# Placing four groups of value products behind chosen projection matmuls, and storing the last output row in equal halves

## The chip, the cores and the metric

The program runs on one core of one Trainium2 chip. The metric is the device time of one execution in microseconds (us). The kernel before takes 954.18 us, the median of three runs that lie between 954.12 and 955.09 us. Below, PE is the matmul engine (TensorE), DVE is VectorE, ACT is ScalarE, POOL is GpSimd and SP is SyncE, which here only issues transfers.

## What is computed

One layer of a hybrid decoder over 1040 tokens (16 learned ones ahead of 1024), with a model width of 1024, in float32:

```python
u = rmsnorm(h, g_pre_mix);  z = u @ w_in            # 1024 -> q 512 | k 128 | v 128 | x 512 | y 512
# B: sliding-window attention, window 128, 8 heads of 64, 2 key/value heads, a sink per head
s = q k^T / 8, masked;  p = exp(s - max) / (sum + exp(sink - max));  attn = p v
# A: causal conv(4) on x, then a gated linear recurrence
r, i = sigmoid(xc w_a + b_a), sigmoid(xc w_x + b_x)
a = exp(-8 r softplus(-lam));  h_t = a h_(t-1) + sqrt(1 - a^2) i xc;  rec = gelu(y) h
h = h + rmsnorm(concat(attn, rec) @ w_out)
h = h + rmsnorm(relu(rmsnorm(h) @ w_ff1)^2 @ w_ff2);  return h[16:]
```

## The kernel before

**Numbers and tiles.** Each float32 operand is split into a high and a low part (`split`, lines 94 to 101: a cast on ACT at line 96 and a subtraction on DVE at line 99). A product is then three matmuls (`mm3`, lines 123 to 132: line 125 high by high, line 128 high by low, line 129 low by high). `project` (lines 257 to 270) multiplies one 128-column chunk of `w_in` with the tokens piece by piece, in a PSUM bank with the tag `acc`, of which there are two. `ALL` has four pieces (272, 256, 256 and 256 tokens, 24 matmuls each), `REAL2` two of 512 tokens.

**Attention and its filling.** The loop at line 752 goes over four pairs of heads j and two halves of the tokens. Each turn issues the scores of (j, half), then one projection as filling (`next_fill`), and then `attend` for the (j, half) of the turn before. The fillings come in the order q1, x1, q2, x2, q3, x3, y0, y1, y2, y3; q stands for queries, x for the input of the recurrence and y for its gate. All but the first few are given a low priority, and so they fill PE where nothing more urgent is ready. After the loop come y2 as filling and `attend(3, 1)`; after the gates of the recurrence (`gates`, line 797) comes y3.

`attend` (lines 642 to 681) works on two groups bp = 0 and 1 of two blocks of 128 tokens each; the text calls a group (j, half, bp). Per group: four transposes of the weights on PE (line 649), the split into `mh` and `ml` on ACT and DVE, four mask selections on POOL (line 653, two of `mh` and two of `ml`), then the **value products**, six matmuls at line 663: one of 512 columns from `mh` and one from `ml`, then two and two of 256 columns (128 for each head). Their result is taken from the PSUM bank by two copies on ACT (line 678) and two additions on DVE (line 679).

**What orders the work.** Each engine runs its instructions in a fixed order. A planner makes that order when the program is built: it takes what is ready by its own reckoning, by priority, which is the order of the source with the lags that the kernel adds. `behind(name, ins)` (line 106) adds a rule to it: `ins` is put later than `name`, with no semaphore where both are on one engine. Before the change one group is placed by such a rule, (3, 1, 1): all six of its matmuls stand behind the first matmul of the third `mm3` of y1 (`begun[1][2]`, lines 668 and 669). `begun[c]` holds the first matmul of each `mm3` of y fill c.

**The conv and y0.** `conv` (line 686) does the causal convolution on DVE: one instruction at line 689 and three at line 694 for chunk 3. Fill y0 is copied out of its two banks by ACT (line 723) into a tile with the tag `d`, which the input of the last convolution holds until its last instruction at line 694.

**The end.** The last product of the feed-forward part ends with `finish_late` (line 1422) for four rows of 128 tokens. Per row: the sum at line 1430 on DVE is preceded by an addition (`combine`, line 1030), ACT squares and takes the root (lines 1393 and 1440), DVE takes the reciprocal and scales the row in two pieces (line 1444), and each piece is stored, one by SP and one by ACT (line 1447). For rows 0 to 2 the pieces are columns 512 to 1023 (SP) and 0 to 511 (ACT). For row 3, the last, they are 256 to 1023 (768 columns, SP) and 0 to 255 (ACT).

Of the kernel before, what the change touches and what calls it, by code (L numbers as in the profile page):

```python
# [17 lines left out]
D = 1024  # L18
# [5 lines left out]
NPAIR = 4  # L24
# [13 lines left out]
def hybrid_layer(  # L38
# [6 lines left out]
    nc = tc.nc  # L45
    x, out = x[0], out[0]
# [11 lines left out]
    def slot(tag, shape, dt=F32):  # L58
        uid[0] += 1
        return slab.tile(shape, dt, tag=tag, name=f"{tag}{uid[0]}", bufs=bufs[tag])  # L60

    def pair(tag, shape):
        return slot(tag, shape, F32R), slot(tag, shape, F32R)

    def bank(tag, shape=(P, 512)):
        uid[0] += 1
        return ps.tile(list(shape), F32, tag=tag, name=f"ps_{tag}{uid[0]}")

    def f32(ap):
        return ap.bitcast(F32)  # L70
# [23 lines left out]
    def split(hi, lo, src, eng=None):  # L94
        if eng is None:
            nc.scalar.copy(hi, src)  # L96
        else:
            eng.tensor_copy(hi, src)
        low = nc.vector.tensor_tensor(lo, src, f32(hi), op=ALU.subtract).ins  # L99
        mark[0] = low.name  # L100
        return low
# [4 lines left out]
    def behind(name, *inss):  # L106
        for ins in inss:
            tc.add_manual_dep(
                ins, name,
                mybir.DependencyInfo(  # L110
                    mybir.DependencyClass.NoSync, mybir.DependencyReason.DATA
                ),
                reason="order",
            )
# [8 lines left out]
    def mm3(dst, lhs, rhs, start, stop):  # L123
        (lh, ll), (rh, rl) = lhs, rhs
        ins = nc.tensor.matmul(  # L125
            dst, lh, rh, start=start, stop=False, skip_group_check=True
        ).ins
        nc.tensor.matmul(dst, lh, rl, start=False, stop=False, skip_group_check=True)  # L128
        last_mm[0] = nc.tensor.matmul(  # L129
            dst, ll, rh, start=False, stop=stop, skip_group_check=True  # L130
        ).ins.name
        return ins
# [124 lines left out]
    def project(w, pieces, sink, begun=None):  # L257
        wh, wl = w
        for t0, n in pieces:
            acc = bank("acc")  # L260
            for kc in range(KC):
                uh, ul = u[kc]
                ins = mm3(
                    acc[:, :n], (wh[:, kc, :], wl[:, kc, :]),
                    (uh[:, t0 : t0 + n], ul[:, t0 : t0 + n]),
                    kc == 0, kc == KC - 1,
                )
                if begun is not None:
                    begun.append(ins)
            sink(acc[:, :n], t0, n)  # L270
# [11 lines left out]
    ALL = [(0, 272), (272, 256), (528, 256), (784, 256)]  # L282
# [41 lines left out]
    last = [None, None]  # L324
# [120 lines left out]
    def new_q():  # L445

        q = pair("b", [P, T])

        def sink_q(acc, t0, n):
            c = slice(t0 - NMETA, t0 - NMETA + n)  # L450
            for h in range(2):
                r, o = HALF[h], HALF[1 - h]
                q_made[:] = split_scaled(q[h][r, c], q[h][o, c], acc[r], HD ** -0.5)

        return q, sink_q

    def new_x(tag="d", c=0):
        xr = slot(tag, [P, TT])
        y = slot("d", [P, TT]) if c == 2 else None

        def sink_x(acc, t0, n):
            nc.scalar.copy(xr[:, t0 : t0 + n], acc)
            if y is not None:
                nc.scalar.activation(
                    y[:, t0 : t0 + n], acc, AF.Identity,
                    scale=prm[:, c, 3:4], bias=prm[:, c, 4:5],
                )

        return xr, sink_x, y
# [172 lines left out]
    def attend(j, half, pairs):  # L642
        g = j // 2
        o_ = slot("e", [P, 512])
        for bp, sn in enumerate(pairs):
            mh, ml = pair("c", [P, 4, 2, P])
            pt = bank("pt", (P, 4, P))
            for k in range(4):
                nc.tensor.transpose(pt[:, k, :], sn[:, k, 0:P], ident)
            split(mh[:, :, 1, :], ml[:, :, 1, :], pt)  # L650
            for m in (mh, ml):
                for side, op, sign in ((0, ALU.is_gt, 1), (1, ALU.is_ge, -1)):
                    nc.gpsimd.affine_select(  # L653
                        out=m[:, :, side, :], in_=f32(m)[:, :, 1, :],
                        pattern=[[0, 4], [-sign, P]], compare_op=op, fill=0.0,
                        base=0, channel_multiplier=sign,
                    )
            po = bank("o", (P, 2, 256))
            mhv, mlv = (m.rearrange("p (h i) s q -> p h (i s q)", h=2) for m in (mh, ml))

            def av(v, oc, n, pc, first, last):
                for k, m in enumerate((mhv, mlv)):
                    ins = nc.tensor.matmul(  # L663
                        po[:, :, oc : oc + n], v, m[:, :, pc : pc + n],
                        start=first and k == 0, stop=last and k == 1,
                        skip_group_check=True,
                    ).ins
                    if (j, half, bp) == (NPAIR - 1, 1, 1):
                        behind(begun[1][2].name, ins)

            b = 4 * half + 2 * bp
            av(vk[g][:, b, :], 0, 256, P, True, False)
            av(vm[:, g, :] if b == 0 else vk[g][:, b - 1, :], 0, P, 0, False, False)
            av(vk[g][:, b + 1, :], P, P, 3 * P, False, True)
            c = slice(256 * bp, 256 * bp + 256)
            for h in range(2):
                r, o = HALF[h], HALF[1 - h]
                nc.scalar.copy(o_[r, c], po[o, h, :])
                nc.vector.tensor_tensor(o_[r, c], po[r, h, :], o_[r, c], op=ALU.add)
        ah, al = at[half][j // 2]  # L680
        split(ah[:, j % 2, :], al[:, j % 2, :], o_)
# [4 lines left out]
    def conv(c, xr, tag="d", y=None):  # L686
        if y is None:
            y = slot(tag, [P, TT])
            nc.vector.tensor_scalar(
                y, xr, prm[:, c, 3:4], prm[:, c, 4:5], op0=ALU.mult, op1=ALU.add  # L690
            )
        for k in (2, 1, 0):
            s = 3 - k
            nc.vector.scalar_tensor_tensor(
                y[:, s:], xr[:, : TT - s], prm[:, c, k : k + 1], y[:, s:],
                op0=ALU.mult, op1=ALU.add,
            )
        xc[c] = y

    ys = [None] * NLRU  # L700
    begun = {}

    def fill_q(j):
        def run(w):
            q, sink = new_q()
            project(w, REAL2, sink)
            qs[j] = q
        return run

    def fill_x(c):  # L710
        def run(w):
            xr, sink, y = new_x(c=c)
            project(w, ALL, sink)
            conv(c, xr, "b" if c == 3 else "d", y)
        return run

# [250 lines left out]
    def out_banks(t):  # L967
        tag = ("pt", "o", "acc", "s", "pt", "acc", "s", "pt")[t]
        return [bank(tag), bank(tag)]
# [190 lines left out]
    for t in range(8):  # L1160
        po = pos[t] if t < 4 else out_banks(t)
# [227 lines left out]
    COLS = (slice(0, 512), slice(512, 1024))  # L1389
# [32 lines left out]
    def finish_late(j, y, parts):  # L1422

        h, o, ssq = halves[j]
        acc = facc["0", j]
        for k, c in enumerate(parts):
            yield k
            last = combine(acc[:, c], y[k], acc[:, c], ALU.add).name
            part = squares(y[k], acc[:, c], k)
            scaled = combine(o[:, c], acc[:, c], gffn_b[:, c], ALU.mult)  # L1430
            if len(parts) == 1:
                behind(last, *held)
                held.clear()
            else:
                behind(scaled.name, held.pop(0))
            if k < len(parts) - 1:
                nc.vector.tensor_tensor(ssq, ssq, part, op=ALU.add)
        root = small.tile([P, 1], F32, name="root", tag="root")
        rs = small.tile([P, 1], F32, name="rs", tag="rs")
        lut(root, part, AF.Sqrt, bias=ssq)  # L1440
        nc.vector.reciprocal(rs, root)
        cut = 256 if j == 3 else 512
        for c, eng in zip((slice(cut, D), slice(0, cut)), (nc.sync, nc.scalar)):
            held.append(nc.vector.scalar_tensor_tensor(
                o[:, c], o[:, c], rs, h[:, c], op0=ALU.mult, op1=ALU.add
            ).ins)
            eng.dma_start(out[j * P : (j + 1) * P, c], o[:, c])
# [102 lines left out]
```

## Time and profile before

| what | value |
| --- | --- |
| median of 3 runs | 954.18 us |
| the profiled execution | 953.82 us |
| its span, first to last instruction | 952.1 us |
| attention with its fillings | up to about 187 us |
| gates, recurrence | about 187 to 240 us |
| output projection, feed-forward | about 225 us to the end |

The profiled execution spent 1.7 us outside its span. All times of day in the text are microseconds from the start of the span. A row of the timeline gives the start, the duration, the engine, the line, the operation, "out<-in" by tile names without their numbers, the shapes, how many instructions are merged in the row, and in brackets how long the engine sat idle before it and what ended that. PE's matmuls overlap, and so the distance between the starts of two rows is what PE spends on one: 0.12 us for 256 columns and 0.23 us for 512. PEq, ACTq and SPq are the engines' own instruction queues.

### The profile page before, as it was taken

To read this page: it belongs to the slowest core of one execution; us is meant where nothing else is said; L and a number is where in the kernel's file an instruction comes from. 1 tells how busy PE (TensorE), PEld (TensorE's weight loads), DVE (VectorE), ACT (ScalarE), POOL (GpSimd) and SP (SyncE) were. 2 spreads that over 40 slices of the span, in tenths; PEclk is the share of its full clock that TensorE was granted. 3 is DMA by queue.
4 is the path that set the end of the run, shared out by engine and by line. 5 is a ranking of instruction groups with operands and counts; after the bars stand their busy time and mean duration, and the time that the engine had idled before them with its cause. 6 is when DMAs were issued, how large, how long until landed. Compare 5 with 4: busy or idle time off the path is not lost.

```text
span 952.1 us, 12444 instructions
## 1 busy us (share of the span) xinstructions
PE 941.1 (99%) x4677; PEld 785.6 (83%) x4677; DVE 681.4 (72%) x966; ACT 499.8 (52%) x824; POOL 154.3 (16%) x196
## 2 busy tenths in 40 slices
PE   9999999999999999999999999999999999999996
PEld 8999999878888877888888888888888888888885
DVE  6679998878966776665655466567667676779874
ACT  7556676579345554433555575663533343445441
POOL 2115665600021100000101001101121100003020
PEclk9999999999999999999999999999999999999999
DMA  8121101203246466675656457645677665556512
GB/s 291 52 54 36 42 5 34 89 24 110 67 168 185 134 208 212 181 262 176 221 177 199 155 185 230 202 157 145 164 178 176 181 217 201 180 194 155 131 46 89
DMA packets 85628, 140.76 MB, mean 148 GB/s; under 512 B 5784, under 2 KB 49064, under 8 KB 85568
## 3 DMA queue, kind: packets, MB, share of 16 engines
q1 hardware_dynamic: 75104, 108.64, 35.6%
q0 software_dynamic: 9600, 29.36, 12.1%
q10 hardware_dynamic: 864, 1.97, 0.6%
q8 instruction: 37, 0.61, 0.3%
q14 instruction: 23, 0.19, 0.1%
HBM read 115.70 MB, written 23.07 MB: 146 GB/s over the span
## 4 chain that ended last, share of the span: by engine, by line
PE 94%; DVE 2%; POOL 2%; ACT 1%; DMA 0%; issue 0%; SPq 0%; DVEq 0%; ACTq 0%; POOLq 0%
PE ps_acc L125 11%; PE ps_acc L128 11%; PE ps_acc L129 11%; PE ps_pt L125 7%; PE ps_pt L129 7%; PE ps_pt L128 6%; PE ps_s L125 6%; PE ps_s L129 6%; PE ps_s L128 6%; PE ps_o L128 5%; PE ps_o L125 5%; PE ps_o L129 5%; POOL c L653 1%; PE ps_o L663 1%; PE ps_o L1004 1%; PE ps_s L602 1%
## 5 line engine op out<-in xcount | busy, mean ns | idle before, releaser
L96 ACT CAST ws<-raw 128x1024 fp32r<-128x1024 f32 (+1 forms) x64 | 65.4, 1022 | 100.7 <-PE ps_o L128 47.1
L99 DVE TENSOR_TENSOR ws<-raw,ws 128x1024 fp32r<-128x1024 f32 (+1 forms) x65 | 78.2, 1203 | 38.0 <-ACT ws L96 37.9
L125 PE MATMUL ps_acc<-a,ws 128*128 128x256 f32 (+2 forms) x256 | 85.7, 335 | 0.0
L129 PE MATMUL ps_acc<-a,ws 128*128 128x256 f32 (+2 forms) x256 | 85.0, 333 | 0.0
L128 PE MATMUL ps_acc<-a,ws 128*128 128x256 f32 (+2 forms) x256 | 84.9, 331 | 0.0
L99 DVE TENSOR_TENSOR b<-b,b 128x1024 fp32r<-128x1024 f32 (+2 forms) x48 | 57.5, 1198 | 27.4 <-PE ps_o L128 22.2
L96 ACT CAST ws<-e 128x1024 fp32r<-128x1024 f32 x41 | 42.9, 1047 | 65.1 <-PE ps_o L128 37.7
L99 DVE TENSOR_TENSOR ws<-e,ws 128x1024 fp32r<-128x1024 f32 x41 | 50.1, 1222 | 26.7 <-ACT ws L96 26.7
L96 ACT CAST b<-b 128x1024 fp32r<-128x1024 f32 (+2 forms) x48 | 49.5, 1030 | 37.6 <-DVE b L1030 34.6
L653 POOL TENSOR_SCALAR_AFFINE_SELECT c<-c 128x512 fp32r<-128x512 f32 x64 | 56.2, 901 | 24.0 <-ACT c L96 20.3
L125 PEld LDWEIGHTS ps_acc<-a,ws 128*128 128x128 f32 x256 | 48.2, 188 | 5.2 <-issue 0.9
L178 POOL TENSOR_TENSOR rs<-ms,half_pow 128x1 f32<-128x1 f32 x26 | 19.4, 750 | 203.2 <-DVE ms L174 202.0
L129 PEld LDWEIGHTS ps_acc<-a,ws 128*128 128x128 f32 x256 | 48.2, 188 | 4.9
L128 PEld LDWEIGHTS ps_acc<-a,ws 128*128 128x128 f32 x256 | 48.1, 188 | 4.3 <-issue 0.2
L125 PE MATMUL ps_acc<-ws,b 128*128 128x512 f32 (+1 forms) x120 | 46.3, 386 | 0.0
L129 PE MATMUL ps_acc<-ws,b 128*128 128x512 f32 (+1 forms) x120 | 46.2, 385 | 0.0
L128 PE MATMUL ps_acc<-ws,b 128*128 128x512 f32 (+1 forms) x120 | 46.1, 384 | 0.0
L128 PE MATMUL ps_pt<-ws,b 128*128 128x512 f32 x112 | 44.0, 393 | 0.0
L125 PE MATMUL ps_pt<-ws,b 128*128 128x512 f32 x112 | 44.0, 394 | 0.0
L129 PE MATMUL ps_pt<-ws,b 128*128 128x512 f32 x112 | 43.9, 392 | 0.0
L125 PE MATMUL ps_s<-ws,b 128*128 128x512 f32 x110 | 43.3, 395 | 0.0
L129 PE MATMUL ps_s<-ws,b 128*128 128x512 f32 x110 | 43.3, 393 | 0.0
(438 smaller groups left out, 2740.5 us busy)
## 6 DMA issues: line engine op xcount, KB each, us to landing
raw<-in_w_ff_dram SPq DMA_DIRECT2D x51, 512.0 KB, 4.3
e<-in_w_ff_dram SPq DMA_DIRECT2D x33, 512.0 KB, 4.2
m<-in_w_ff_dram SPq DMA_DIRECT2D x16, 512.0 KB, 4.7
raw<-in_w_in_dram SPq DMA_DIRECT2D x12, 512.0 KB, 5.3
d<-in_w_ff_dram SPq DMA_DIRECT2D x12, 512.0 KB, 4.6
s_dram<-d POOLq DMA_DIRECT2D x12, 512.0 KB, 3.9
raw<-in_w_ff_dram POOLq DMA_DIRECT2D x10, 512.0 KB, 5.7
e<-in_w_ff_dram POOLq DMA_DIRECT2D x9, 512.0 KB, 5.7
```

Source lines behind the costliest of these rows:

```text
L96: nc.scalar.copy(hi, src)
L99: low = nc.vector.tensor_tensor(lo, src, f32(hi), op=ALU.subtract).ins
L125: ins = nc.tensor.matmul(dst, lh, rh, start=start, stop=False, skip_group_check=True).ins
L128: nc.tensor.matmul(dst, lh, rl, start=False, stop=False, skip_group_check=True)
L129: last_mm[0] = nc.tensor.matmul(dst, ll, rh, start=False, stop=stop, skip_group_check=True).ins.name
L178: last_pow[0] = nc.gpsimd.tensor_tensor(rs[:n], ms[:n], half_pow[:n], op=ALU.pow).ins.name
L602: nc.tensor.matmul(dst, q[h][:, c], lo, start=False, stop=True, skip_group_check=True,)
L653: nc.gpsimd.affine_select(out=m[:, :, side, :], in_=f32(m)[:, :, 1, :], pattern=[[0, 4], [-sign, P]], compare_op=op, fill=0.0, base=0, cha ...
L663: ins = nc.tensor.matmul(po[:, :, oc : oc + n], v, m[:, :, pc : pc + n], start=first and k == 0, stop=last and k == 1, skip_group_check=Tr ...
L1004: nc.tensor.transpose(pt[:, i, :], xn[:, kc * P : (kc + 1) * P], ident)
```

## The change

Four groups of value products get a place behind a projection matmul, through a table. The key is (j, half, bp); the value names the fill and the number of the `mm3` in it, counted from 0. `begun` is kept for the x fills too. (3, 1, 1) moves from the third `mm3` of y1 to the sixth. The last row is scaled and stored in pieces of 512 columns, as the rows before it.

```diff
-            def av(v, oc, n, pc, first, last):
+            def av(v, oc, size, pc, first, last):
                 for k, m in enumerate((mhv, mlv)):
                     ins = nc.tensor.matmul(
-                        po[:, :, oc : oc + n], v, m[:, :, pc : pc + n],
+                        po[:, :, oc : oc + size], v, m[:, :, pc : pc + size],
...
-                    if (j, half, bp) == (NPAIR - 1, 1, 1):
-                        behind(begun[1][2].name, ins)
+                    if (j, half, bp) in AV_BEHIND:
+                        c, n = AV_BEHIND[j, half, bp]
+                        behind(begun[c][n].name, ins)
...
+    AV_BEHIND = {(0, 1, 1): (("x", 1), 9), (2, 1, 1): (("x", 3), 4), (3, 1, 0): (1, 2), (3, 1, 1): (1, 5)}
...
             xr, sink, y = new_x(c=c)
-            project(w, ALL, sink)
+            begun["x", c] = []
+            project(w, ALL, sink, begun["x", c])
...
-        cut = 256 if j == 3 else 512
-        for c, eng in zip((slice(cut, D), slice(0, cut)), (nc.sync, nc.scalar)):
+        for c, eng in zip(COLS[::-1], (nc.sync, nc.scalar)):
```

## The prediction

> **What bounds the kernel.** I read the page first, then the waits of PE, then the value products (line 663) alone in three stretches: one in which nothing waits, and the two with PE's waits.
>
> ```profile
> span 952.1 us, 12444 instructions
> PE 941.1 (99%) x4677; PEld 785.6 (83%) x4677; DVE 681.4 (72%) x966; ACT 499.8 (52%) x824; POOL 154.3 (16%) x196
> PE   9999999999999999999999999999999999999996
> PE 94%; DVE 2%; POOL 2%; ACT 1%; DMA 0%; issue 0%; SPq 0%; DVEq 0%; ACTq 0%; POOLq 0%
> PE ps_o L663 <- POOL c L653: 1.0, 2, 0.5
> 122.34:123.26 0.92, 0.92 (x6) 1.00 0.00 0
> 150.13:152.76 2.63, 2.12 (x12) 1.00 0.08 17
> 181.77:183.44 1.67, 1.19 (x6) 1.00 0.00 0
> ```
>
> PE is the bound: busy for 941.1 of 952.1 us and 94% of the chain that ended last. So an edit that only changes PE's order can gain no more than PE's gaps, and the value products have two. The waits name 1.0 us in two waits, but a matmul's modelled end hides part of each. The last three rows (stretch, length, busy time, count, clock) show it: six products that wait for nothing take 0.92 us. Twelve took 2.63, so 2.63 - 1.84 = **0.79 us** is lost there; six took 1.67, so **0.75 us** is lost. Together 1.54 us, 0.16% of the time.
>
> **First tie, (0, 1, 1).** PE's rows around x1 and this group:
>
> ```profile
> 81.97 0.37 PE L125 MATMUL ps_acc<-a,ws 128*128 128x272 f32 x1
> 87.83 0.28 PE L125 MATMUL ps_acc<-a,ws 128*128 128x256 f32 x1
> 99.82 0.40 PE L663 MATMUL ps_o<-c,b 128*128 128x512 f32 x1
> ```
>
> Fill x1 begins at 81.97. Its tenth `mm3` opens with its 28th matmul, the row at 87.83. The group's first product comes at 99.82, 12.0 us behind that. The rule already holds: 0 us, and no queue changes.
>
> **Second tie, (2, 1, 1).** PE, then POOL's last selection for the group:
>
> ```profile
> 150.13 1.33 PE L663 MATMUL ps_o<-c,b 128*128 128x512 f32 x7
> 151.96 0.98 PE L663 MATMUL ps_o<-c,b 128*128 128x512 f32 x5 [0.50 <-POOL c L653]
> 152.77 0.29 PE L125 MATMUL ps_acc<-a,ws 128*128 128x272 f32 x1
> 154.27 0.29 PE L125 MATMUL ps_acc<-a,ws 128*128 128x272 f32 x1
> 150.28 1.63 POOL L653 TENSOR_SCALAR_AFFINE_SELECT c<-c 128x512 fp32r<-128x512 f32 x1
> ```
>
> The seven products are (2, 1, 0) whole and the first of (2, 1, 1). The eighth waits for POOL, until 150.28 + 1.63 = 151.91. Behind it stands x3, from 152.77. With the tie 13 matmuls of x3 come first: the 13th is at 154.27, so 1.50 + 0.12 = 1.62 us of work. (2, 1, 0) ends at 150.13 + 0.92 = 151.05, x3's part at 152.67, and by then POOL is done. PE saves 0.79 us here; x3's bank and weights were at hand, or it costs what they are late. The two ACT copies and two DVE additions of (2, 1, 1) come later: its products end at 152.67 + 0.92 = 153.59, not at 152.77 (+0.82 us).
>
> **Third and fourth tie, (3, 1, 0) and (3, 1, 1).** PE, POOL, DVE and ACT:
>
> ```profile
> 181.53 0.40 PE L129 MATMUL ps_acc<-a,ws 128*128 128x512 f32 x1
> 181.77 0.39 PE L663 MATMUL ps_o<-c,b 128*128 128x512 f32 x1
> 182.64 0.98 PE L663 MATMUL ps_o<-c,b 128*128 128x512 f32 x5 [0.48 <-POOL c L653]
> 183.45 0.40 PE L125 MATMUL ps_acc<-a,ws 128*128 128x512 f32 x1
> 186.23 0.86 PE L663 MATMUL ps_o<-c,b 128*128 128x512 f32 x5
> 180.95 1.63 POOL L653 TENSOR_SCALAR_AFFINE_SELECT c<-c 128x512 fp32r<-128x512 f32 x1
> 182.54 0.63 POOL L653 TENSOR_SCALAR_AFFINE_SELECT c<-c 128x512 fp32r<-128x512 f32 x1
> 180.75 1.34 DVE L694 SCALAR_TENSOR_TENSOR b<-d,prm,b 128x1037 f32<-128x1037 f32 x1
> 182.12 0.59 ACT L723 COPY d<-ps_acc 128x512 f32<-128x512 f32 x1 [1.50 <-DVE b L694]
> ```
>
> Fill y0 ends with the row at 181.53. The first product of (3, 1, 0) goes at 181.77, the second waits for the selection that ends at 182.58, and y1 starts at 183.45. The tie puts y1's first seven matmuls ahead of the group. But **can y1 start at 181.77?** It needs one of two `acc` banks, and y0 holds both: its first half is copied out at 182.12, after ACT has waited 1.50 us for the last conv instruction (180.75 + 1.34 = 182.09), whose input holds y0's tile. The bank is free at 182.12 + 0.59 = 182.71. So the wait for POOL is exchanged for a wait for the bank: before, y1 stood at 183.45 with the group done; now it starts at about 182.71 with the group's 0.92 us still to do, the equal of 183.63. That is **0.18 us worse**, if the conv stays where it is.
>
> Does it stay? What stands between the second tie and the conv:
>
> ```profile
> 166.98 0.48 DVE L618 CUSTOM_DVE_ANT_0 c<-ps_s,m,nsink 128x256 f32<-128x256 f32 x1 [1.02 <-PE ps_s L602]
> 167.51 0.51 ACT L82 ACTIVATE c<-c,negm 128x257 f32<-128x257 f32 x1 [0.44 <-DVE negm L618]
> ```
>
> DVE waits 1.02 us for the last scores from PE, and ACT then 0.44 us for DVE. With PE 0.79 us earlier, ACT's queue, which carries the evictions that the conv waits for, can move 0.44 us and no more. I take 0.44: the conv ends, and y1 starts, 0.44 us earlier, and PE is ahead by 0.44 - 0.18 = **0.26 us** from here on. The ends: 0.79 passes whole (0.61 us gained), or nothing (0.18 us lost). The rest of the 0.79 goes into a longer gap ahead of y1.
>
> (3, 1, 1), now behind 16 matmuls of y1 and the other group, ends at 182.71 - 0.44 + 16 x 0.24 + 2 x 0.92 = 188.0 us, against 186.23 + 0.92 - 0.24 = 186.9 (0.24 us is the pitch of 512 columns: 181.77 less 181.53; the last five products follow the row at 186.23). Who waits for that 1.1 us comes with the rivals.
>
> **The tail.** DVE's scaling of an ordinary row and of the last, the stores, and what the DMA engines moved:
>
> ```profile
> 936.96 1.40 DVE L1444 SCALAR_TENSOR_TENSOR a<-a,rs,d 128x512 f32<-128x512 f32 x2
> 946.39 1.41 DVE L1444 SCALAR_TENSOR_TENSOR a<-a,rs,d 128x768 f32<-128x768 f32 x2
> out_dram<-a SPq DMA_DIRECT2D x3, 256.0 KB, 2.1
> out_dram<-a SPq DMA_DIRECT2D x1, 384.0 KB, 2.4
> out_dram<-a ACTq DMA_DIRECT2D x1, 128.0 KB, 3.3
> 949.00:949.50 0.50, 0.00 (x0) 0.00 (x0) 0.00 (x0) 0.00 (x0) 0.00 (x0) 0.50 0.94 344
> 949.50:950.00 0.50, 0.00 (x0) 0.00 (x0) 0.00 (x0) 0.00 (x0) 0.00 (x0) 0.50 0.39 137
> ```
>
> Two halves take DVE 1.40 us, 768 and 256 columns 1.41: the second piece is scaled at the same moment, and ACT issues its store as before. SP's store goes out about 0.3 us earlier (0.70 of 1.40, not about 1.0 of 1.41) and is 128 KB smaller; ACT's is 128 KB larger. All 16 DMA engines are 94% busy until 949.5 with the same 512 KB, so I take **0 us**. Ends: from 0.3 us gained (the data begin that much sooner) to 0.3 lost (384 KB took 2.4 us, 256 KB 2.1, and the ACT store is the one that lands last).
>
> [...]
>
> **Sum.** 0 - 0.26 + 0 = -0.26 us. On the profiled execution, 953.82 us, that gives 953.56; on the median of 954.18 it gives **953.9 us**.
>
> **The rivals.** The rows for them, four of ACT, then DVE and PE:
>
> ```profile
> 152.97 0.37 ACT L678 COPY e<-ps_o 64x256 f32<-64x256 f32 x1 [1.29 <-PE ps_o L663]
> 154.21 0.59 ACT L117 ACTIVATE b<-ps_acc 64x512 fp32r<-64x512 f32 x1 [0.86 <-DVE b L118]
> 188.84 0.62 ACT L96 CAST b<-e 128x512 fp32r<-128x512 f32 x1 [0.49 <-DVE e L679]
> 189.37 2.02 ACT L96 CAST b<-d 128x1040 fp32r<-128x1040 f32 x2
> 190.83 2.38 DVE L99 TENSOR_TENSOR b<-d,b 128x1040 fp32r<-128x1040 f32 x2
> 193.48 0.42 PE L808 MATMUL ps_s<-b,b 64*128 64x348 f32 x1
> ```
>
> *A, both gaps covered.* If the planner lets ACT empty y0's bank sooner, or finds PE other work for the second gap, 0.79 + 0.75 = 1.54 us are gained, and with the tail's good end 1.84: 952.3 us. Against it: the bank hangs on the conv, which the change doesn't touch.
>
> *B, slower: the late copies hold up ACT's queue.* ACT already waited 1.29 us at 152.97 for a value product, with the eviction of q3 (154.21) behind it. If the planner leaves that copy ahead, it now waits 0.82 us longer, and the scores, the exponentials and the conv behind it move too. Then y1's bank is free 0.82 us later, not 0.44 earlier: 0.18 + 0.82 = 1.0 us lost. At the second place the cast of this group's output (188.84) stands ahead of the casts for the gates (189.37), whose first low part DVE ends at about 190.83 + 1.19 = 192.0; the gates' first matmul is at 193.48. The products now end at 182.71 + 0.82 + 16 x 0.24 + 1.84 = 189.2, 2.3 us late, so the low part comes at 194.3; the gates' matmul, 1.0 us late, is due at 194.5. Of 1.5 us of cover 0.2 are left, and one more DVE instruction of 1.2 us in between makes PE wait 1.0 us. With the tail's bad end that is 1.0 + 1.0 + 0.3 = 2.3 us: 956.5. It decides once ACT's order keeps the copies ahead. For it: ACT waited there before; against it: the planner knows of the rule and may deal the queue anew.
>
> *C, nothing of it arrives.* The conv stays, or the planner orders something else differently: 0.18 us lost, 954.4, in the forecast's own range.
>
> *D, the larger last store lands later.* 128 KB more took SP 2.4 - 2.1 = 0.3 us. If that falls on the end, the sum is 0.04 us slower, 954.2. For it: ACT's store lands last, and it is the one that grows. Against it: SP's store is smaller and earlier by as much, on the same 16 engines. [...]
>
> *E, the planner re-deals the order far from here*, by more than 1.9 us either way. PE is busy for 9 tenths or more in 39 of 40 slices (its row on the page), so there is little to gain, and more to lose.
>
> **How the numbers follow.** A measurement of this kernel tells some 0.2%, 1.9 us, from no change. The forecast alone 0.33, C 0.12, D 0.13: together 0.58 (-0.61 - 0.3 to +0.18 + 0.3 us, 953.3 to 954.7), all within 0.2%. A: 0.12, to 952.3; its full size is 1.84 us, so a third of it, 0.04, is counted beyond 1.9. B: 0.22, of which 0.16 beyond 1.9 us. E: 0.03 faster and 0.05 slower. Faster 0.04 + 0.03 = 0.07, slower 0.16 + 0.05 = 0.21, within 0.72. The range takes in A and B: 952.3 to 956.5.
>
> **What would show it.** In the profile after: the products of (2, 1, 1) behind 13 matmuls of x3 without a wait; PE idle ahead of y1 from 181.77 - 0.79 = 180.98 to 182.71 - 0.44 = 182.27, for 1.3 us, released by ACT at line 723 and not by POOL; x1's part unchanged; the last matmul about 0.3 us earlier, and from there to the end of the span as long as before. I am wrong if y1 starts right behind y0, if ACT or the gates' first matmul waits longer, or if PE has new gaps after 190 us.

## The result, and the profile after

The changed kernel takes **951.74 us**, the median of 15 runs (951.03 to 953.91), beside 954.34 us of the kernel before (15 runs, 953.58 to 955.87). The ratio is **0.9974, with a 95% interval of 0.9966 to 0.9981**: 2.5 us or 0.26% faster. The forecast was 953.9 us and its range began at 952.3, so the forecast was wrong. The profiled execution of after took 951.04 us with a span of 949.4, which is 2.8 us less than that of before.

First the page of after: its span, the busy times, PE's share in 40 slices, and the shares of the chain that ended last. Then the one line that the waits of PE give between 60 and 400 us (engine, tile and line, what it waited for, us in total, times, longest).

```profile
span 949.4 us, 12443 instructions
PE 940.6 (99%) x4677; PEld 786.5 (83%) x4677; DVE 681.3 (72%) x966; ACT 499.9 (53%) x824; POOL 155.1 (16%) x196
PE   9999999999999999999999999999999999999997
PE 97%; DVE 1%; DMA 0%; ACT 0%; POOL 0%; issue 0%; DVEq 0%; SPq 0%
```

```profile
PE ps_acc L125 <- ACT a L1233: 0.7, 1, 0.7
```

The waits of value products for POOL are gone from the list. What is left is at line 1233, far behind the change; before had the same 0.7 us at line 1229. POOL's 2% of the chain is gone too. PE has the same 4677 matmuls and nearly the same busy time: the work is as it was, and the gaps went.

**Where the 2.8 us went.** The last matmul splits the span into PE's part and the tail. The first row is of before, the second of after.

```profile
944.42 0.28 PE L129 MATMUL ps_acc<-a,b 128*128 128x256 f32 x1
```

```profile
942.92 0.28 PE L129 MATMUL ps_acc<-a,b 128*128 128x256 f32 x1
```

The last matmul begins 1.50 us earlier, and the time from there to the end of the span falls from 952.12 - 944.42 = 7.70 to 949.36 - 942.92 = 6.44 us, by 1.26 us (spans here to two places, as the trace has them). The forecast had 0.26 and 0.

**The second tie, on PE.** Fill x3 and group (2, 1, 1), from the timeline of after:

```profile
151.08 0.29 PE L125 MATMUL ps_acc<-a,ws 128*128 128x272 f32 x1
152.58 0.28 PE L125 MATMUL ps_acc<-a,ws 128*128 128x272 f32 x1
152.71 1.10 PE L663 MATMUL ps_o<-c,b 128*128 128x512 f32 x6
153.65 0.28 PE L128 MATMUL ps_acc<-a,ws 128*128 128x272 f32 x1
```

Thirteen matmuls of x3 run from 151.08 to 152.71, and the six products follow in 0.94 us with no bracket, that is, without a wait. This is the picture that the forecast drew.

**The third and fourth tie, on PE.** Around the change from y0 to y1, in after:

```profile
181.07 0.40 PE L129 MATMUL ps_acc<-a,ws 128*128 128x512 f32 x1
181.30 0.49 PE L125 MATMUL ps_acc<-a,ws 128*128 128x512 f32 x1
182.78 0.39 PE L125 MATMUL ps_acc<-a,ws 128*128 128x512 f32 x1
183.01 0.39 PE L663 MATMUL ps_o<-c,b 128*128 128x512 f32 x1
184.41 0.40 PE L125 MATMUL ps_acc<-a,ws 128*128 128x512 f32 x1
186.71 0.86 PE L663 MATMUL ps_o<-c,b 128*128 128x512 f32 x5
```

Here the forecast drew PE idle for 1.3 us, waiting for y0's bank. But y1 begins at 181.30, one pitch behind the last matmul of y0; PE loses 0.10 us there (y1's second matmul is at 181.63, where a pitch of 0.23 would give 181.53). The six products of (3, 1, 0) begin behind seven matmuls of y1, at 183.01, and go on without a wait; the last row holds the last five of (3, 1, 1). The bank was free in time. The reason stands in DVE's queue, below as it was before (first fence) and is after (second fence), and in ACT's copy of y0 out of its first bank (third fence, after).

```profile
178.04 1.28 DVE L694 SCALAR_TENSOR_TENSOR b<-d,prm,b 128x1038 f32<-128x1038 f32 x1
179.35 0.88 DVE L679 TENSOR_TENSOR e<-ps_o,e 64x256 f32<-64x256 f32 x2
180.15 0.67 DVE L99 TENSOR_TENSOR c<-ps_pt,c 128x512 fp32r<-128x512 f32 x1
```

```profile
177.20 1.29 DVE L695 SCALAR_TENSOR_TENSOR b<-d,prm,b 128x1038 f32<-128x1038 f32 x1
178.41 0.41 DVE L680 TENSOR_TENSOR e<-ps_o,e 64x256 f32<-64x256 f32 x1
179.34 1.28 DVE L695 SCALAR_TENSOR_TENSOR b<-d,prm,b 128x1037 f32<-128x1037 f32 x1
180.54 0.86 DVE L680 TENSOR_TENSOR e<-ps_o,e 64x256 f32<-64x256 f32 x2
181.76 0.69 DVE L99 TENSOR_TENSOR c<-ps_pt,c 128x512 fp32r<-128x512 f32 x1 [0.35 <-ACT c L96]
```

```profile
180.65 0.59 ACT L727 COPY d<-ps_acc 128x512 f32<-128x512 f32 x1 [1.44 <-DVE b L695]
```

(Lines behind the edits are numbered one to four higher in after.) Before, the last conv instruction stood behind two additions and the low part of (3, 1, 1)'s weights, and ran at 180.75. In after it stands ahead of them, and runs at 179.34. The conv is 1.47 us sooner (182.09 to 180.62), ACT's copy is 1.47 us sooner (182.12 to 180.65), and the bank is free at 181.24, before y1 wants it. No line of the conv is in the diff: the planner dealt DVE's queue anew. It dealt others anew too: on ACT, the copy of (2, 1, 1) that waited 1.29 us for a value product at 152.97 in before, ahead of q3's eviction (154.21), stands at 158.62 in after.

**The tail.** When SP issues its piece of the last row, in before and then in after; and from the DMA issues of after, how long the last row's two stores took (tile, queue, count, KB of one, us to landing):

```profile
947.44 0.33 SPq L1447 DMA_DIRECT2D out_dram<-a  x1
```

```profile
945.67 0.33 SPq L1450 DMA_DIRECT2D out_dram<-a  x1
```

```profile
out_dram<-a SPq DMA_DIRECT2D x1, 256.0 KB, 2.1
out_dram<-a ACTq DMA_DIRECT2D x1, 256.0 KB, 2.0
```

SP issues 947.44 - 944.42 = 3.02 us behind the last matmul's begin in before, and 2.75 in after: 0.27 us sooner, the 0.3 of the forecast's good end. And ACT's last store, with twice the bytes, takes 2.0 us where the smaller one took 3.3. The experiments take these two apart.

### The profile page after: what moved, and what is told of

Same layout as the page of the kernel before. It is cut to its first block, busy times and chain, and to the rows that moved or that the text cites. A ratio compares the mean times of both kernels' runs of the same rounds, so it can differ in the third digit from the quotient of the medians.

```text
span 949.4 us, 12443 instructions
## 1 busy us (share of the span) xinstructions
PE 940.6 (99%) x4677; PEld 786.5 (83%) x4677; DVE 681.3 (72%) x966; ACT 499.9 (53%) x824; POOL 155.1 (16%) x196
## 4 chain that ended last, share of the span: by engine, by line
PE 97%; DVE 1%; DMA 0%; ACT 0%; POOL 0%; issue 0%; DVEq 0%; SPq 0%
PE ps_acc L125 12%; PE ps_acc L128 12%; PE ps_acc L129 12%; PE ps_pt L125 7%; PE ps_pt L129 7%; PE ps_pt L128 7%; PE ps_s L125 6%; PE ps_s L129 6%; PE ps_s L128 6%; PE ps_o L125 5%; PE ps_o L128 5%; PE ps_o L129 5%; PE ps_o L663 2%; PE ps_s L602 1%; PE ps_s L598 1%; PE ps_o L1008 1%
```

## The experiments

Three questions were open: which tie gave the 1.5 us, whether it came through DVE's queue or through PE's own order, and what shortened the tail. Of every run the trace gives the time from the third value product (the row at 80.20 in before) to the begin of the last matmul, "PE's part" below. It leaves out the start-up, which ran 1.6 us late in the profiled executions of two of the kernels. The tail is again from that begin to the end of the span.

| run | PE's part, us | tail, us | ratio to before, 95% interval |
| --- | --- | --- | --- |
| before | 864.22 | 7.70 | |
| after | 862.71 | 6.44 | 0.9974 [0.9966, 0.9981] |
| tail_alone | 864.09 | 7.48 | 0.9996 [0.9987, 1.0005] |
| second_tie_alone | 862.85 | 6.79 | 0.9978 [0.9969, 0.9986] |
| last_ties_alone | 864.21 | 7.70 | 0.9998 [0.9989, 1.0006] |
| no_first_tie | 863.14 | 6.44 | 0.9972 [0.9962, 0.9983] |
| tie_no_redeal | 863.88 | 7.30 | 0.9994 [0.9986, 1.0003] |
| conv_late | 868.46 | 6.44 | 1.0029 [1.0019, 1.0039] |
| cover_first | 862.82 | 6.45 | 0.9974 [0.9965, 0.9983] |
| before_more_dve | 864.39 | 6.78 | 0.9991 [0.9982, 1.0000] |
| after_more_dve | 862.98 | 7.44 | 0.9982 [0.9973, 0.9991] |
| before_dve_halves | 864.68 | 6.44 | 0.9989 [0.9980, 0.9998] |

PE's part of kernels with the same order on PE differs by up to 0.6 us from profile to profile, so a difference of 0.3 us there says little by itself; those of 1.4 do.

**tail_alone.** The kernel before with only the halves:

```diff
-        cut = 256 if j == 3 else 512
-        for c, eng in zip((slice(cut, D), slice(0, cut)), (nc.sync, nc.scalar)):
+        for c, eng in zip(COLS[::-1], (nc.sync, nc.scalar)):
```

> The kernel before with the last row in equal halves and nothing else. Theory T (the tail gave about 1.2 us, because the store that lands last took 3.3 us with 256 columns and 2.0 us with 512): ratio to before about 0.9988, 1.1 us faster; from the last matmul's end to the end of the span 6.2 us instead of 7.4. Rival R (the shorter tail of the one profile was chance, and all of the gain comes from the ties): within 0.3 us of before, ratio 0.9997 to 1.0003.

Measured: 953.69 us, ratio 0.9996, and a tail of 7.48 us: 0.22 shorter than before, where after is 1.26 shorter. So the halves alone don't give the tail of after; something in the other parts of the change does.

**second_tie_alone** and **last_ties_alone.** Both have the rule read from a table, as after has it, and the tail of before. The first of the two tables is that of second_tie_alone, the second that of last_ties_alone:

```diff
-                    if (j, half, bp) == (NPAIR - 1, 1, 1):
-                        behind(begun[1][2].name, ins)
+                    if (j, half, bp) in AV_BEHIND:
+                        c, n = AV_BEHIND[j, half, bp]
+                        behind(begun[c][n].name, ins)
...
+    AV_BEHIND = {(2, 1, 1): (("x", 3), 4), (3, 1, 1): (1, 2)}
```

```diff
+    AV_BEHIND = {(3, 1, 0): (1, 2), (3, 1, 1): (1, 5)}
```

> The kernel before with the tie of (2, 1, 1) behind the fifth mm3 of x3 added and nothing else: (3, 1, 1) stays behind the third mm3 of y1, (3, 1, 0) gets no rule, the tail is that of before. Theory T (this tie alone makes the planner deal DVE's queue anew, so that the conv ends 1.4 us sooner and y1 follows y0 at once): 1.5 us faster, ratio 0.9984, no wait of PE for POOL in the value products of (3, 1). Rival R (the tie fills its own gap of 0.79 us, and the third and fourth tie fill the other): 0.8 us faster, ratio 0.9992, and 0.7 us still lost ahead of y1.

Measured: 951.76 us, ratio 0.9978. The second tie alone brings nearly all: PE's part is 1.37 us shorter, and the tail 0.91. Its order of instructions is that of after on every engine but for the first product of (3, 1, 1), which stands three matmuls earlier; so the re-dealt DVE queue comes from the second tie, and the tie of (3, 1, 0) adds nothing once it is there.

> The kernel before with the third and fourth tie (both groups of (3, 1)) and without the first two; the tail is that of before. The prediction's bank argument: PE waits ahead of y1 from 181.8 until ACT's copy of y0 ends at about 182.7, and the time is 0.2 us slower than before, ratio 1.0002. Rival (the tie by itself covers the wait for POOL): y1 starts at 181.8 without a wait, 0.75 us faster, ratio 0.9992.

Measured: 953.82 us, ratio 0.9998, PE's part unchanged. The waits of PE and y1's first matmul in this run:

```profile
PE ps_acc L125 <- ACT d L727: 0.8, 1, 0.8
```

```profile
182.65 0.50 PE L125 MATMUL ps_acc<-a,ws 128*128 128x512 f32 x1 [0.83 <-ACT d L727]
```

With the conv where it was, y1 waits for ACT's copy and begins at 182.65; the forecast worked out 182.71 for it. The wait for POOL became a wait for the bank, and nothing was gained. The argument about the bank was right, and its condition (the conv stays) was what failed.

**no_first_tie.** After without (0, 1, 1):

```diff
-    AV_BEHIND = {(0, 1, 1): (("x", 1), 9), (2, 1, 1): (("x", 3), 4), (3, 1, 0): (1, 2), (3, 1, 1): (1, 5)}
+    AV_BEHIND = {(2, 1, 1): (("x", 3), 4), (3, 1, 0): (1, 2), (3, 1, 1): (1, 5)}
```

> The changed kernel without the first tie, that of (0, 1, 1). As the prediction has it, the rule already held and changes nothing: the time of the changed kernel, 2.6 us faster than before, ratio 0.9966 to 0.9981. If the first tie matters, up to 0.5 us less of a gain.

Measured: 951.39 us, ratio 0.9972, with the same order of instructions on every engine as after. The first tie is inert, as forecast.

**tie_no_redeal.** The second tie, but behind the second `mm3` of x3 instead of the fifth, the last tie as in before, no other; the tail of after. In this program DVE's last conv instruction stays behind the low part of (3, 1, 1)'s weights:

```diff
-    AV_BEHIND = {(0, 1, 1): (("x", 1), 9), (2, 1, 1): (("x", 3), 4), (3, 1, 0): (1, 2), (3, 1, 1): (1, 5)}
+    AV_BEHIND = {(2, 1, 1): (("x", 3), 1), (3, 1, 1): (1, 2)}
```

> The second tie stands earlier (behind the 2nd mm3 of x3 instead of the 5th) and the third and first are left out, (3, 1, 1) stays where it was before; the tail is that of after. In this program's order of instructions DVE's last convolution instruction stays behind the low part of (3, 1, 1)'s weights, as before the change. Theory (the gain of the ties came from the re-dealt DVE queue, not from PE's order): the second gap of about 0.75 us ahead of the products of (3, 1, 0) stays, and the last matmul begins 0.0 to 0.8 us earlier than in the kernel before (about 944.1), not 1.5; ratio 0.998 to 1.000. Rival (PE's own order gives the gain wherever DVE's queue stands): the last matmul begins about 1.5 us earlier, at 942.9, as in after. On the tail, by the theory of the instruction fetch: 7.4 us from the last matmul's begin to the end of the span if the packet of the instruction queue falls within 5.6 us of it, 6.4 if it comes later.

Measured: 953.63 us, ratio 0.9994, PE's part 863.88, which is 0.34 us shorter than in before and not 1.5. First its products of (2, 1, 1) with the matmul behind them, and those of (3, 1, 0); then DVE's last conv instruction and what stands ahead of it (all times 1.6 us late, by the start-up):

```profile
153.19 1.36 PE L663 MATMUL ps_o<-c,b 128*128 128x512 f32 x6
154.39 0.29 PE L128 MATMUL ps_acc<-a,ws 128*128 128x272 f32 x1
...
183.86 0.97 PE L663 MATMUL ps_o<-c,b 128*128 128x512 f32 x5 [0.47 <-POOL c L653]
```

```profile
180.58 0.88 DVE L680 TENSOR_TENSOR e<-ps_o,e 64x256 f32<-64x256 f32 x2
181.38 0.67 DVE L99 TENSOR_TENSOR c<-ps_pt,c 128x512 fp32r<-128x512 f32 x1
181.98 1.33 DVE L695 SCALAR_TENSOR_TENSOR b<-d,prm,b 128x1037 f32<-128x1037 f32 x1
```

The products of (2, 1, 1) take 1.20 us up to the next matmul, so of 0.79 us lost 0.28 are left: a gain of 0.5 at its place. The second gap is there as before, with its wait for POOL. A tie of the same kind, dealt without the new DVE queue, leaves the second gap open. Its 0.34 us is near the forecast's 0.26, but that is no test of the 0.26: the ties are others, and PE's part differs by more from profile to profile.

**conv_late.** After, with the last conv instruction put back behind the low part of (3, 1, 1)'s weights on DVE:

```diff
-            split(mh[:, :, 1, :], ml[:, :, 1, :], pt)
+            low = split(mh[:, :, 1, :], ml[:, :, 1, :], pt)
+            if (j, half, bp) == (3, 1, 1):
+                behind(low.name, conv_last[0])
...
+    conv_last = [None]
...
-            nc.vector.scalar_tensor_tensor(
+            conv_last[0] = nc.vector.scalar_tensor_tensor(
...
-            )
+            ).ins
```

> The changed kernel with one more rule: the last instruction of the convolution of chunk 3 stands on DVE behind the low part of the weights of group (3, 1, 1), as in the kernel before, where the planner had put it there. Theory T (y1 can follow y0 at once only because the planner now deals the conv ahead of that): PE waits ahead of y1 for ACT's copy of y0, for about 0.7 to 1.3 us, and that much of the gain is lost, ratio 0.9980 to 0.9986. Rival (PE's earlier arrival alone does it): no wait ahead of y1, the gain of the changed kernel, ratio 0.9973.

Measured: 956.84 us, ratio 1.0029, 0.29% slower than before, and PE's part 5.75 us longer than in after. PE's timeline, and two stretches of its windows (length, busy time, count, granted clock, DMA's share, GB/s):

```profile
184.60 0.79 PE L125 MATMUL ps_acc<-a,ws 128*128 128x512 f32 x1 [3.16 <-ACT d L731]
185.19 0.63 PE L128 MATMUL ps_acc<-a,ws 128*128 128x512 f32 x1
185.62 0.63 PE L129 MATMUL ps_acc<-a,ws 128*128 128x512 f32 x1
...
187.75 1.91 PE L665 MATMUL ps_o<-c,b 128*128 128x512 f32 x6
...
190.30 0.39 PE L125 MATMUL ps_acc<-a,ws 128*128 128x512 f32 x1
190.53 0.40 PE L128 MATMUL ps_acc<-a,ws 128*128 128x512 f32 x1
```

```profile
186.40:189.80 3.40, 3.40 (x11) 0.50 0.50 154
190.40:192.00 1.60, 1.60 (x9) 1.00 0.00 0
```

y1 begins at 184.60 instead of 181.30, and waits for the bank, so the place of the conv in DVE's queue does decide it. The price expected was 0.7 to 1.3 us. That it became 5.75 has two causes. The conv came out later than in before: the low part ahead of it ran at 182.03 (180.15 in before), so that the conv ended at 183.93 (182.09 in before) and ACT's copy began at 183.96. DVE in this run:

```profile
182.03 0.69 DVE L99 TENSOR_TENSOR c<-ps_pt,c 128x512 fp32r<-128x512 f32 x1
182.64 1.29 DVE L699 SCALAR_TENSOR_TENSOR b<-d,prm,b 128x1037 f32<-128x1037 f32 x1
```

And after 3.16 us without work PE ran at half its clock: the rows are 0.43 us apart instead of 0.23, and the granted clock is 0.50 up to 190.30. The 15 matmuls of these 5.70 us need 9 x 0.23 + 0.92 = 2.99 at the full clock, so 2.7 us are the clock's, and 184.60 - 181.30 = 3.3 us the wait's. The experiment shows the direction; as a measure of the undone re-dealing it is too large, and tie_no_redeal is the better one.

The windows of this run bound the moment at which the clock fell: it is 1.00 from 170.00 to 181.00 and 0.50 from 184.00 to 187.00, so it fell between the two, at most 3.0 us behind the begin of y0's last matmul (181.04). It came back at about 190.3 (0.61 from 189.80 to 190.40, 1.00 from 190.40 on), after PE had been busy for 5.7 us.

**cover_first.** After, with a tie for (0, 0, 1) as well, where PE lost 0.3 us in before, a third and smaller gap (its first product begins at 87.14, 0.41 us behind the scores ahead of it; the pitch of 256 columns is 0.12):

```diff
-    AV_BEHIND = {(0, 1, 1): (("x", 1), 9), (2, 1, 1): (("x", 3), 4), (3, 1, 0): (1, 2), (3, 1, 1): (1, 5)}
+    AV_BEHIND = {(0, 0, 1): (("x", 1), 9), (0, 1, 1): (("x", 1), 9), (2, 1, 1): (("x", 3), 4), (3, 1, 0): (1, 2), (3, 1, 1): (1, 5)}
```

> The changed kernel with a fifth tie: (0, 0, 1), the group whose first product waits for POOL at 86.8, behind the tenth mm3 of x1. Theory (a gap that other work can fill is gained whole, if no engine's queue changes): the 0.44 us between the scores and x1 there go, 0.4 us faster than the changed kernel, ratio to before about 0.9969. Rival (the group's late evictions hold up the scores, which come next): no gain or a loss of up to 0.5 us, ratio 0.9973 to 0.9978.

Measured: 951.44 us, ratio 0.9974, the same as after. Its waits of PE have a new line:

```profile
PE ps_acc L125 <- DVE b L118: 0.4, 1, 0.4
```

The matmuls of x1 that were to cover the gap now wait for their own bank, which DVE empties. This is the exchange that the forecast expected of the third tie, and here it takes place.

**before_more_dve, after_more_dve and before_dve_halves.** With the tail's 1.26 us not in the halves, the DMA packets of the tail were read one by one. In before, a packet of queue q14, which the profile calls "instruction" (the fetch, below), falls among the last store's packets; in after it comes 1.7 us later, behind the end of the span. Both profiles have such packets throughout, 23 and 22 in the span. The rows of the two pages, before and then after (packets, MB, share):

```profile
q14 instruction: 23, 0.19, 0.1%
```

```profile
q14 instruction: 22, 0.18, 0.1%
```

The second tie's program has two DVE instructions fewer (1216 instead of 1218, with those that only wait or signal). So the theory was that the moment of this fetch hangs on the number of DVE's instructions. To move it, one-column memsets of an unused tile were added on DVE at the start: twelve to the kernel before (before_more_dve), two to after (after_more_dve, the same lines with 2 for 12), and twelve to the kernel before with the halves of tail_alone (before_dve_halves):

```diff
+    spare = const.tile([P, 1], F32, name="spare")
+    for _ in range(12):
+        nc.vector.memset(spare, 0.0)
```

> The kernel before with 12 memsets of one column on DVE among its first instructions; every engine's order is otherwise that of before. It computes the same. Theory F (one fetch of DVE instructions falls among the packets of the last store in the kernel before, and holds its end up by 0.9 us; 12 instructions more move that fetch ahead of the last row): the span from the last matmul's end shrinks from 7.4 to about 6.5 us and the time falls by 0.9 us, ratio 0.9990, though DVE has more to do. Rival N (the landing times of 3.3 and 2.0 us are chance of the transfers): the time of before, ratio 1.0000, and landing times that don't follow the place of the fetch.

> The changed kernel with 2 memsets of one column on DVE among its first instructions, which gives DVE's queue as many instructions as in the kernel before; the order is otherwise that of the changed kernel. It computes the same. Theory F: the fetch is back among the last store's packets, from the last matmul's end to the end of the span 7.2 us instead of 6.2, and the gain shrinks from 2.6 to 1.6 us, ratio 0.9983. Rival N: the gain stays at 2.6 us, ratio 0.9973.

> The kernel before with its order, 12 one-column memsets on DVE at the start and the last row in equal halves; no tie. If the two parts of the tail add up (the instruction fetch out of the last store's way 0.9 us, equal halves 0.3 us), the span ends 6.4 to 6.5 us after the last matmul begins, 1.2 to 1.3 less than before (7.70), with the last matmul where it was before (944.4, about 0.3 later for the memsets); ratio about 0.9988. Rival (the two overlap, and halves only mattered through the moment of the fetch): 6.8 us as in the run with the memsets alone; ratio 0.9991.

Measured: twelve instructions more made the kernel before **not slower** (953.23 us, ratio 0.9991; the interval reaches 1.0000, so the times alone don't show that it got faster), with a tail of 6.78 us instead of 7.70. Two more gave after a tail of 7.44 instead of 6.44, and 952.48 us. And twelve with the halves gave 6.44, to the hundredth the tail of after, without any tie (0.9989). For all twelve kernels, worked out from the DMA packets of the traces, in us from the last matmul's begin ("none": with 1230 instructions the fetch falls 22.5 us ahead of that begin):

| DVE instructions | last row in | kernels | q14 packet at | the store's last packet ends at | tail |
| --- | --- | --- | --- | --- | --- |
| 1218 | 768 and 256 | before, last_ties_alone | 5.38, 5.38 | 5.95, 5.95 | 7.70, 7.70 |
| 1218 | halves | tail_alone, after_more_dve, tie_no_redeal | 5.03, 5.11, 4.96 | 6.03, 5.80, 5.85 | 7.48, 7.44, 7.30 |
| 1216 | 768 and 256 | second_tie_alone | 7.44 | 5.37 | 6.79 |
| 1216 | halves | after, no_first_tie, cover_first, conv_late | 7.07 to 7.10 | 5.11 | 6.44, 6.44, 6.45, 6.44 |
| 1230 | 768 and 256 | before_more_dve | none | 5.37 | 6.78 |
| 1230 | halves | before_dve_halves | none | 5.11 | 6.44 |

The stores' data end at 5.37 us with 768 and 256 columns and at 5.11 with halves, and some packets end 0.6 to 0.9 us behind that wherever the fetch falls among them, in no other run. The late packets start as the fetch's packet ends: in before it lasts 0.31 us, from 5.38 to 5.69, and the store's last three data packets start at 5.69, 5.73 and 5.80. How it looks: the end of the last store in tail_alone (0.9 us in 40 slices, each digit the packets' time in tenths of the 16 DMA engines' slice, a packet's whole time in the slice where it starts; then the packets, MB and share of a queue) and in after (1.5 us):

```profile
DMA  7992997645429000000000000000000000020004
q10 hardware_dynamic: 57, 0.09, 26.3%
q14 instruction: 1, 0.01, 3.8%
```

```profile
DMA  7959597996610000000000000000000000000000
q10 hardware_dynamic: 90, 0.15, 26.5%
```

In tail_alone the 9 in the 13th slice (949.17) is the fetch, a packet of 0.54 us. For the next 0.5 us no data packet of the store starts, and then single ones 0.5 and 0.6 us behind it (the 2 and the 4). In after the row ends clean. And by the landing of ACT's last store, in tail_alone, before_more_dve and after_more_dve in this order (x2 counts the store of the row before as well; the view has a landing for the last one alone):

```profile
out_dram<-a ACTq DMA_DIRECT2D x2, 256.0 KB, 3.1
```

```profile
out_dram<-a ACTq DMA_DIRECT2D x1, 128.0 KB, 2.4
```

```profile
out_dram<-a ACTq DMA_DIRECT2D x2, 256.0 KB, 3.0
```

The same 128 KB that took 3.3 us in before land in 2.4 when the fetch is out of the way, and the 256 KB of after take 3.0 when it is put in the way. The two parts of the tail add up: by the table 0.92 us are the fetch's (7.70 to 6.78) and 0.34 the halves' (6.78 to 6.44; 6.79 to 6.44 is 0.35). The late packets account for 0.6 to 0.9 us of what the fetch costs in a trace; the 0.1 to 0.3 us that the kernel's end loses beyond them stay unexplained. Each tail is that of one profile, but kernels of the same row of the table agree within 0.2 us. The timed ratios go the same way, though each difference of less than 1 us lies within its interval.

That the packet is a fetch of DVE's instructions is the author's reading of the queue's name and of the table, where its moment goes with their number; no view shows what it carries. In after q14 moves 0.18 MB in 22 packets, 8 KB each. On the last store of before it was not hidden: the tail is 0.92 us shorter without it there (7.70 to 6.78).

No version here beats after clearly: no_first_tie, with 951.39, has the same order, and cover_first, with 951.44, lies within its interval.

## Why the prediction was wrong

- **PE is the bound, and 1.54 us in two gaps is what an order can gain:** right. PE's part got 1.50 us shorter.
- **First tie, 0 us:** right (no_first_tie).
- **Second tie, 0.79 us at its place:** right, in the picture and in the size.
- **Third and fourth tie, "0.18 us worse, if the conv stays where it is":** the condition is shown in both directions. Where the conv stays (last_ties_alone), y1 begins within 0.06 us of the time worked out, released by ACT at the copy of y0. Where it moves, both gaps go.
- **"With PE 0.79 us earlier, ACT's queue ... can move 0.44 us and no more. I take 0.44":** this is the step that failed on PE. By it PE was to gain 0.26 us; PE's part got 1.50 us shorter, and y1 started right behind y0, which the forecast had named as a sign of being wrong. The step took the order of DVE's queue as fixed and asked only how far the same instructions slide. The planner put the last conv instruction ahead of two additions and a low part (0.88 + 0.67 us of DVE before), and the first conv instruction ran at 170.27 instead of 170.90; the instructions in between took 0.6 us longer, and 1.47 us came of it at the conv's end. The working had the means to see the sensitivity: one of the three instructions ahead of the conv was the low part of a tied group's weights, and rival A's condition ("if the planner lets ACT empty y0's bank sooner") is word for word what happened. It was held to be unlikely because the change doesn't touch the conv; that speaks against an edit of the conv, not against a new place for it. Why the planner deals so at the fifth `mm3` of x3 and not at the second was not found out, and no run moves the conv alone in the kernel before: that its place is needed is shown, that it would do without the second tie is not.
- **The tail, 0 us with ends of 0.3:** the second step that failed, wrong in the ends; the tail got 1.26 us shorter. The halves gave 0.22 to 0.34, the good end, through SP's earlier issue. The other 0.92 us was a transfer that no part of the diff names: a packet of the queue "instruction". The forecast bounded the tail by the stores of the kernel alone, while the row "q14 instruction" stood on the page of before, and ACT's small store had taken 3.3 us beside 2.1 to 2.4 for larger ones. That was the one number of the tail that didn't fit, and it was quoted and not asked about.
- **Rival D, the larger store lands later:** didn't happen. By the 2.4 and 2.1 us that 384 and 256 KB took on SP's queue in before, the larger store was to cost an estimated 0.3 us more. The traces differ: ACT's 256 KB landed in 2.0 us (after), its 128 KB in 2.4 without the fetch (before_more_dve). Both stores share the 16 engines (from 949.0 to 949.5 in before, SP's packets took 56.1% of their time and ACT's 37.5%), and the 0.26 us by which the data end sooner are the 0.27 by which SP issues sooner.
- **Rival A** is what PE did, at nearly its full 1.54 us, and with the fetch the whole went beyond its 1.84. **Rival B** didn't happen: the gates' first matmul comes 0.9 us later (194.41 beside 193.48), but PE works through to it without a wait, and ACT's queue, on which B hung, was dealt anew (the copy at 152.97 went behind). **C** was wrong with the forecast. **E**, a new deal far away, didn't show.
- **Of the chances**, 0.07 on faster was too little: a gap of known size, with the planner free to deal anew, deserved more than rival A's 0.12.

## What to carry to other kernels

Where a planner makes the order, an edit's effect on the engines that it doesn't name can be as large as on the one that it does: compare the order of instructions on every engine before reasoning with the old queues, and where that can't be seen, give a new deal a real share of the chance. A bank held by a copy that waits for an unrelated instruction is worth following: here 1.47 us of DVE's order decided whether the second gap of 0.75 us closed or not. And at the end of a kernel, read every DMA queue of the last few microseconds, those of the instructions too; a landing that is longer than that of a larger neighbour is a question, not a constant.

## What was not expected of the hardware

- One packet of 8 KB on q14, the queue "instruction", among the last store's packets delayed some of them by 0.6 to 0.9 us and the end of the kernel by 0.9 to 1.0; two DVE instructions more or fewer decided it.
- One wait of 3.16 us cost PE 2.7 us more at a granted clock of 0.50; the clock fell at most 3.0 us behind the begin of the matmul ahead of the wait. Behind the kernel's last matmul it fell 2.3 us after that matmul's begin in after (granted clock 0.79 from 945.00 to 945.40) and 4.4 in before (0.75 from 948.50 to 949.20), so no fixed time shows. Between 0.8 us (last_ties_alone, without such a loss) and 3.16 no run has a wait there.
